# Attention scores and a chunk scan contracted over all 128 rows, with masks added by VectorE

## The chip, the cores and the metric

One core of a Trainium2 chip runs the whole kernel as one program. The metric is the device time of that program in microseconds (us), from its start to its end. A core has a matrix engine (TensorE, PE in the profile; its weight loads are PEld), three engines for element-wise work (VectorE or DVE, ScalarE or ACT, GpSimd or POOL), an engine that starts transfers (SyncE or SP), and DMA queues between the chip's memory (HBM) and the on-chip memories: SBUF, from which engines read and which has 128 rows (partitions), and PSUM, into which TensorE writes. A matrix multiplication on TensorE contracts over the rows: it takes a stationary operand (loaded as weights) and a moving one, both with the contracted index on the rows.

## The reference, cut to what matters

Two transformer blocks run one after the other on 256 tokens of width 1024, all in float32. Block 1 has two attentions side by side (branch a: 8 heads of width 64; branch b: 8 heads whose queries and keys are 96 wide), and a feed-forward layer that gathers experts. Block 2 has two layers: the first mixes tokens by a gated unit and a gated delta rule (a scan over 4 chunks of 64 tokens, 4 heads of width 128), the second by a differential attention: 8 heads, each with two maps of width 64, whose logits get a slope times the distance. What bears on the change:

```python
# branches a and b (one key block covers all 256 tokens)
s = einsum('bhqd,bhkd->bhqk', q, k) * scale
p = softmax(where(k_pos <= q_pos, s, -inf))          # then p @ v

# the differential attention
dist   = q_pos[:, None] - k_pos[None, :]
logits = einsum('bqhrd,bkhrd->bhrqk', q_blk, k) - slopes * dist     # slopes: 2 ** -(head + 1)
probs  = softmax(where(dist >= 0, logits, -inf))
attn   = probs[:, :, 0] - lam * probs[:, :, 1]       # then attn @ v

# one chunk of the scan
v_new = u_c - einsum('bhck,bhkv->bhcv', w_c, state)
o_c   = einsum('bhck,bhkv->bhcv', q_c, state) + einsum('bhij,bhjv->bhiv', qk_c, v_new)
state = state * gl_c + einsum('bhck,bhcv->bhkv', k_c, v_new)
```

## The kernel before, in words

The code is written stage by stage, and a tile framework orders each engine's instructions by its own cost model and by which buffers are free; `issue_after` holds an instruction back until another is issued. So the order on an engine isn't that of the code: between the attention heads TensorE also has passes of big matrix products (`gemm_steps`, whose float32 precision is made of three products of split weights, lines 83 to 85), and VectorE and ScalarE have the splits of their weights (lines 77 and 78). Two PSUM pools of four buffers feed this: `mm_tile` for scores and transposes, `acc_tile` for the products' sums.

**Scores.** The 256 queries make two tiles of 128. For a head, `scores` (lines 289 to 301) fills three blocks of 128 columns of one PSUM tile: queries 0 against keys 0, queries 1 against keys 0, queries 1 against keys 1. In branch a and the differential attention a head (or map) is 64 wide: two of them lie one above the other in the 128 rows of `qaT`, `kaT` and `qkT` (named `dT` in the profile), and a matmul (line 295) reads only the 64 rows of its own. In branch b the operands have 96 rows. The mask is added by a further matmul in bf16 (line 297): the identity times the mask (`identb`, `cmb`), and in the differential attention the identity times the head's slope (`idh`) times the distances (`cb`, named `c1bb` in the profile). VectorE takes the negated row maxima (lines 299 and 300), ScalarE the exponentials from PSUM with their sums (`exps`, lines 303 to 305), each followed by an instruction that reads the sum's accumulator. `pv` (lines 307 to 316) transposes the probabilities on TensorE (line 310), lets ScalarE copy them (line 312) and multiplies by the values (lines 313 to 315). One head is worked ahead: the scores of head h + 1 stand in front of the transposes of head h.

**Around the scores.** In branch a `transposes_a` writes q^T and k^T, each by one ScalarE copy for every two pairs of heads; branch b's are copied by VectorE (line 465). In the differential attention `head_tr` does it (lines 1306 and 1307), half of the heads before head 0 and half after head 1's scores; `head_s` forms both maps of a head and combines them on VectorE (lines 1346 to 1350).

**The scan.** Two tiles of 128 tokens hold the four chunks of 64. Chunk c reads rows `rw` (the upper or lower 64) of tile c // 2: line 1076 multiplies the state (128 rows), line 1081 makes the state's update over the 64 rows of the chunk, lines 1093 and 1094 make the chunk's output in turn over 128 rows and 64 rows, head by head. `kdec` (named `kd`) holds the scaled keys, one tile per 128 tokens, made by `scaled` (line 966) on ScalarE ahead of the scan, as are `kbg` and the others.

Of the kernel before, what the change touches and what calls it, by code (L numbers as in the profile page):

```python
# [40 lines left out]
C_CM, C_D0, C_D1 = 0, 128, 256  # L41
C1_COLS = 384
# [6 lines left out]
def kernel(ctx: ExitStack, tc: tile.TileContext, A: dict, out: bass.AP):  # L49
# [239 lines left out]
    def scores(qT, kT, name, masks, w):  # L289

        s = mm_tile(name + "s")
        for o, q, k in ((0, 0, 0), (1, 1, 0), (2, 1, 1)):
            c = slice(o * P, o * P + P)
            m = masks[o]
            PE.matmul(s[:, c], qT[:, q * P : q * P + P], kT[:, k * P : k * P + P], start=True, stop=m is None)
            if m is not None:
                PE.matmul(s[:, c], w, m, start=False, stop=True)
        nm = sm.tile([P, 2], F32, tag="nmx", name=name + "m")
        V.tensor_reduce(nm[:, 0:1], s[:, 0:P], AX.X, OP.max, negate=True)
        V.tensor_reduce(nm[:, 1:2], s[:, P : 3 * P], AX.X, OP.max, negate=True)  # L300
        return s, nm

    def exps(s, nm, p, sums):
        S.activation(p[:, 0:P], s[:, 0:P], AF.Exp, bias=nm[:, 0:1], accum_out=sums[:, 0:1])
        return S.activation(p[:, P : 3 * P], s[:, P : 3 * P], AF.Exp, bias=nm[:, 1:2], accum_out=sums[:, 1:2])
# [13 lines left out]
    with tc.tile_pool(name="p1", bufs=1) as p1:  # L319
# [13 lines left out]
        c1 = p1.tile([P, P], F32, name="c1")  # L333
        cmb = p1.tile([P, P], BF16, name="cmb")
# [33 lines left out]
        nc.sync.dma_start(c1, A["c1"][:, C_CM : C_CM + P])  # L368
        nc.sync.dma_start(fin, A["rows"][:, R_FIN : R_FIN + D].to_broadcast((P, D)))
        V.tensor_copy(cmb, c1)  # L370
# [48 lines left out]
        qaT = p1.tile([P, 4, T], F32, name="qaT")  # L419
        kaT = p1.tile([P, 4, T], F32, name="kaT")  # L420

        def transposes_a(i, dst, sc):
# [3 lines left out]
            for g in range(2):  # L426
# [5 lines left out]
                S.activation(dst[:, 2 * g : 2 * g + 2], tp.rearrange("p (j t) -> p j t", j=2), AF.Copy, scale=sc)  # L432

        transposes_a(0, qaT, 0.125)
# [16 lines left out]
        transposes_a(1, kaT, 1.0)  # L451
# [20 lines left out]
        def attention(br, fill):  # L472
# [3 lines left out]
            for h in range(8 + AHEAD):  # L476
                if h < 8:
                    if br == "a":
                        qT, kT = (z[h % 2 * 64 : h % 2 * 64 + 64, h // 2, :] for z in (qaT, kaT))
                    else:  # L480
                        qT, kT = qbT[:, h, :], kbT[:, h, :]
                    s, nm = scores(qT, kT, f"at{br}{h}", (cmb, None, cmb), identb)
                    p = p1.tile([P, 3 * P], F32, tag="p", name=f"p{br}{h}", bufs=AHEAD + 1)
                    last_exp[:] = [exps(s, nm, p, sums[:, h, :])]
# [269 lines left out]
    with tc.tile_pool(name="p3", bufs=1) as p3:  # L754
# [16 lines left out]
        def v4(ps):  # L771
            return ps.rearrange("p (h d) -> p h d", h=4)
# [184 lines left out]
        V.tensor_mul(beg, beta, egc)  # L957

# [76 lines left out]
        for t in range(2):  # L1035
            kdec.append(scaled(f"kd{t}", ktok[t], ekd[:, t]))
# [29 lines left out]
        for c in range(4):  # L1066
# [4 lines left out]
            else:  # L1071
# [18 lines left out]
            for hd in range(4):  # L1090
# [3 lines left out]
                PE.matmul(oh, qkD[t][rw, hd], vn[rw, hd], start=st is None, stop=True)  # L1094
# [65 lines left out]
    with tc.tile_pool(name="p4", bufs=1) as p4_:  # L1160
# [3 lines left out]
        qkT = [p4_.tile([P, 8, T], F32, name=f"dT{i}") for i in range(2)]  # L1164
# [84 lines left out]

        c1 = p4_.tile([P, C1_COLS], F32, name="c1b")  # L1250
        nc.sync.dma_start(c1, A["c1"])
# [4 lines left out]
        cb = p4_.tile([P, C1_COLS], BF16, name="c1bb")  # L1256
        idh = [p4_.tile([P, P], BF16, name=f"idh{i}") for i in range(8)]
# [41 lines left out]
        def head_tr(i, hf):  # L1299
            gain = aq if i == 0 else gcols[:, G_AK : G_AK + 1]  # L1300
            for g in range(2):
                tp = mm_tile(f"td{i}{hf}{g}")
                for j in range(2):
                    for t in range(2):
                        b = hf * 512 + (2 * g + j) * P
                        PE.transpose(tp[:, j * T + t * P : j * T + t * P + P], qk[i][t][:, b : b + P], ident)
                S.activation(qkT[i][:, hf * 4 + 2 * g : hf * 4 + 2 * g + 2], tp.rearrange("p (j t) -> p j t", j=2), AF.Copy,
                             scale=gain)
# [211 lines left out]
```

## Time and profile before

| what | value |
|---|---|
| median of three runs | 1772.1 us (1767.64 to 1775.27) |
| the profiled execution's own time | 1771.07 us |
| its span in the trace | 1769.3 us |
| mean granted clock of TensorE | .997 of full speed |
| TensorE busy | 1731.0 us, 98% of the span |
| VectorE busy | 1132.1 us, 64% |
| ScalarE busy | 876.1 us, 50% |
| GpSimd busy | 0.8 us, 10 instructions |
| moved by DMA | 321.28 MB, mean 182 GB/s |

An engine's busy time counts the instructions that work on data. Matmuls are pipelined: in a row of equal ones each starts before the one ahead has ended, so the duration of one is longer than the distance of two starts. A float32 matmul is recorded as two passes; "x2" in a row of the timeline means two records of one form that follow each other, and its duration goes from the first start to the last end. The stages of this case lie at about 72 to 96 us (branch a), 113 to 137 us (branch b), 1149 to 1169 us (scan) and 1467 to 1526 us (differential attention).

### The profile page before, as it was taken

How to read it: one execution, taken by the hardware profiler on the slowest of the kernel's cores; microseconds unless marked ns; L12 is line 12 of the kernel's file. 1: busy time of each engine (PE TensorE's matmuls, PEld its weight loads, DVE VectorE, ACT ScalarE, POOL GpSimd, SP SyncE). 2: the span in 40 equal slices, each digit the busy share in tenths (PEclk: the TensorE clock that was granted, in tenths of full speed). 3: DMA queues.
4: the chain of work that ended last, by engine and by line, in shares of the span. 5: the costliest groups of instructions: out<-in, count | busy, mean ns of one | idle time of the engine just before them, and what ended most of it. 6: DMA issues, size and time to landing. Idle time of an engine off the chain costs nothing.

```text
span 1769.3 us, 26510 instructions
## 1 busy us (share of the span) xinstructions
PE 1731.0 (98%) x10846; PEld 1508.3 (85%) x10846; DVE 1132.1 (64%) x1867; ACT 876.1 (50%) x1146; POOL 0.8 (0%) x10
## 2 busy tenths in 40 slices
PE   8999999999999999999999999999999999999998
PEld 7788899899999999998888887878998787689996
DVE  6646699999656565555555597656555666665555
ACT  5654544555444444444444477535444565454444
POOL 0000000000000000000000000000000000000000
PEclk9999999999999999999999999999999999999999
DMA  6424445477777777765555543215555552255552
GB/s 234 140 96 146 173 152 178 150 275 286 254 253 247 247 248 247 245 211 190 191 190 190 183 156 120 96 48 194 190 189 189 173 179 96 81 177 179 184 191 95
DMA packets 83066, 321.28 MB, mean 182 GB/s; under 512 B 9472, under 2 KB 44544, under 8 KB 47104
## 3 DMA queue, kind: packets, MB, share of 16 engines
q1 hardware_dynamic: 82944, 319.58, 53.0%
q8 instruction: 85, 1.39, 0.3%
q14 instruction: 37, 0.30, 0.0%
HBM read 301.72 MB, written 17.83 MB: 181 GB/s over the span
## 4 chain that ended last, share of the span: by engine, by line
PE 91%; DVE 5%; ACT 3%; DMA 1%; issue 1%; SPq 0%; DVEq 0%; ACTq 0%
PE pv L85 7%; PE pv L83 7%; PE pv L84 7%; PE m L84 3%; PE m L85 3%; PE m L83 3%; PE gp L717 2%; PE wia L84 1%; PE wia L85 1%; PE wia L83 1%; PE pt L92 1%; PE pj L1180 1%; PE wda L83 1%; PE wda L85 1%; PE wda L84 1%
## 5 line engine op out<-in xcount | busy, mean ns | idle before, releaser
L740 ACT ACTIVATE wh<-ga 128x512 fp32r<-128x512 f32 x64 | 40.4, 632 | 194.9 <-PE pv L84 194.9
L741 DVE TENSOR_TENSOR wl<-ga,wh 128x512 fp32r<-128x512 f32 x64 | 44.2, 693 | 91.6 <-ACT wh L740 91.6
L1200 ACT ACTIVATE ah<-mr 128x512 fp32r<-128x512 f32 x32 | 20.2, 631 | 76.8 <-DVE mr L1197 76.8
L712 DVE TENSOR_TENSOR oh<-oh,gT 128x1024 f16<-128x1024 f16 x64 | 42.3, 687 | 5.3 <-PE gp L717 5.3
L737 DVE TENSOR_TENSOR ga<-ga,gt 128x512 f32<-128x512 f32 x64 | 41.2, 686 | 5.5 <-DMA gt<-gd 5.4
L1201 DVE TENSOR_TENSOR al<-mr,ah 128x512 fp32r<-128x512 f32 x32 | 22.2, 692 | 21.6 <-ACT ah L1200 21.6
L720 ACT ACTIVATE stg<-gp 128x512 f32<-128x512 f32 x64 | 32.9, 608 | 0.0
L717 PE MATMUL gp<-oh,oh 128*128 128x128 f16 x512 | 32.5, 219 | 0.0
L717 PEld LDWEIGHTS <-oh 128*128 128x128 f16 x512 | 29.4, 97 | 0.8
L92 PE MATMUL pt<-c,x 128*128 128x128 f32 x128 | 21.7, 295 | 6.9 <-DMA x<-x 5.3
L92 PEld LDWEIGHTS pt<-c,x 128*128 128x128 f32 x128 | 16.1, 150 | 12.2 <-issue 6.3
L78 DVE TENSOR_TENSOR wiw_0l<-wiw,wiw_0h 128x2048 fp32r<-128x2048 f32 x7 | 16.0, 2291 | 11.5 <-ACT wiw_0h L77 11.5
L83 PE MATMUL wia<-wiw_0h,gh 128*128 128x512 f32 x56 | 22.6, 406 | 0.0
L84 PE MATMUL wia<-wiw_0l,gh 128*128 128x512 f32 x56 | 22.5, 402 | 0.0
L100 ACT ACTIVATE gh<-pt,gcols 128x256 fp32r<-128x256 f32 x32 | 13.0, 475 | 19.0 <-PE pt L92 19.0
L85 PE MATMUL wia<-wiw_0h,gl 128*128 128x512 f32 x56 | 22.3, 398 | 0.0
L709 DVE TENSOR_TENSOR oh<-iotaR,i1T 128x1024 f16<-128x1024 f16 x32 | 22.0, 686 | 0.2 <-PE gp L717 0.2
L84 PE MATMUL wia<-wiw_1l,gh 128*128 128x512 f32 x56 | 22.1, 394 | 0.0
L85 PE MATMUL wia<-wiw_1h,gl 128*128 128x512 f32 x56 | 22.0, 394 | 0.0
L1197 DVE TENSOR_TENSOR mr<-mr 128x512 f32<-128x512 f32 x32 | 21.9, 685 | 0.1
L83 PE MATMUL wia<-wiw_1h,gh 128*128 128x512 f32 x56 | 21.8, 389 | 0.0
L78 DVE TENSOR_TENSOR wdw_0l<-wdw,wdw_0h 128x2048 fp32r<-128x2048 f32 x6 | 13.8, 2293 | 12.2 <-ACT wdw_0h L77 11.9
(2913 smaller groups left out, 6689.7 us busy)
## 6 DMA issues: line engine op xcount, KB each, us to landing
u<-eu SPq DMA_DIRECT2D x64, 1024.0 KB, 5.0
v<-ev SPq DMA_DIRECT2D x64, 1024.0 KB, 4.9
m<-w_mlp SPq DMA_DIRECT2D x64, 1024.0 KB, 4.9
gd<-stg SPq DMA_DIRECT2D x16, 1024.0 KB, 3.9
gt<-gd SPq DMA_DIRECT2D x256, 64.0 KB, 4.5
wiw<-w_in SPq DMA_DIRECT2D x14, 1024.0 KB, 4.8
wdw<-w_qkv SPq DMA_DIRECT2D x12, 1024.0 KB, 4.8
q<-w_query SPq DMA_DIRECT2D x8, 1024.0 KB, 4.9
```

The lines of the kernel that those rows point to most:

```text
L78: V.tensor_sub(lo[:, :n], w[:, :n], hi[:, :n].bitcast(F32)),
L83: PE.matmul(o, ah, bh, start=start, stop=False)
L84: PE.matmul(o, ah, bl, start=False, stop=False)
L85: PE.matmul(o, al, bh, start=False, stop=stop)
L92: PE.transpose(pt[:, t * P : t * P + P], src[t][:, k * P : k * P + P], ident)
L712: V.tensor_tensor(oh[2 + i], oh[1], tok(gT[i]), OP.mult)
L717: PE.matmul(ps[:, i * P : i * P + P], oh[0][:, 2 * g + i // 2, :, i % 2], oh[2 + m][:, 2 * g + i // 2, :, i % 2], start=m == 0, stop=m == 1)
L720: S.activation(stg[:, :, c : c + 4], ps.rearrange("p (t n) -> p n t", t=4), AF.Copy, scale=2.0 ** -15)
L737: V.tensor_tensor(w4, w4, gts[q][:, :, 2 * jj : 2 * jj + 2, :].rearrange("p g j t -> p j g t"), OP.mult)
L740: S.activation(wh, w, AF.Copy)
L741: V.tensor_sub(wl, w, wh.bitcast(F32))
L1201: V.tensor_sub(al, r, ah.bitcast(F32))
```

## The change

There are three parts. First, `scores` makes two matmuls, of 128 and of 256 columns, both over all 128 rows in branch a and the differential attention. For this q^T is kept in two tiles: one has the upper heads' 64 rows and zeros below, the other the lower ones' and zeros above. GpSimd writes the zeros; ScalarE copies each half of a transpose's result to its own tile. k^T stays whole. Second, the masks are no matmuls: VectorE's `tensor_tensor_reduce` adds a float32 mask to the scores in PSUM, negates the sum, writes it to the tile in SBUF that will hold the probabilities, and forms the row minimum, which is the negated maximum. In the program this is one instruction and a second one that reads the accumulator. The exponential then runs in place with scale -1. In the differential attention GpSimd makes the head's mask (`ali`, 128 by 384) from the distances and the head's slope, in two alternating buffers. Third, `kdec` has three tiles, one per chunk that updates the state, whose other 64 rows are zero (the factors `ekc` are masked by columns of `blk`), and all matmuls and subtractions of the scan go over 128 rows.

```diff
-    def scores(qT, kT, name, masks, w):
+    def scores(qT, kT, name, mask, p):
         s = mm_tile(name + "s")
-        for o, q, k in ((0, 0, 0), (1, 1, 0), (2, 1, 1)):
-            c = slice(o * P, o * P + P)
-            m = masks[o]
-            PE.matmul(s[:, c], qT[:, q * P : q * P + P], kT[:, k * P : k * P + P], start=True, stop=m is None)
-            if m is not None:
-                PE.matmul(s[:, c], w, m, start=False, stop=True)
+        PE.matmul(s[:, 0:P], qT[:, 0:P], kT[:, 0:P], start=True, stop=True)
+        PE.matmul(s[:, P : 3 * P], qT[:, P : 2 * P], kT[:, 0 : 2 * P], start=True, stop=True)
         nm = sm.tile([P, 2], F32, tag="nmx", name=name + "m")
-        V.tensor_reduce(nm[:, 0:1], s[:, 0:P], AX.X, OP.max, negate=True)
-        V.tensor_reduce(nm[:, 1:2], s[:, P : 3 * P], AX.X, OP.max, negate=True)
-        return s, nm
+        for i, c in enumerate((slice(0, P), slice(P, 3 * P))):
+            V.tensor_tensor_reduce(p[:, c], s[:, c], mask[:, c], -1.0, 3.0e38, OP.add, OP.min, nm[:, i : i + 1])
+        return nm
-    def exps(s, nm, p, sums):
-        S.activation(p[:, 0:P], s[:, 0:P], AF.Exp, bias=nm[:, 0:1], accum_out=sums[:, 0:1])
...
+    def exps(nm, p, sums):
+        S.activation(p[:, 0:P], p[:, 0:P], AF.Exp, bias=nm[:, 0:1], scale=-1.0, accum_out=sums[:, 0:1])
...
-        c1 = p1.tile([P, P], F32, name="c1")
-        cmb = p1.tile([P, P], BF16, name="cmb")
+        c1 = p1.tile([P, 3 * P], F32, name="c1")
...
-        qaT = p1.tile([P, 4, T], F32, name="qaT")
+        qaT = [p1.tile([P, 4, T], F32, tag=("qaT", "yha")[i], name=f"qaT{i}") for i in range(2)]
+        for i in range(2):
+            GP.memset(qaT[i][64 - 64 * i : 128 - 64 * i], 0.0)
...
-                S.activation(dst[:, 2 * g : 2 * g + 2], tp.rearrange("p (j t) -> p j t", j=2), AF.Copy, scale=sc)
+                for r, d in dst:
+                    S.activation(d[r, 2 * g : 2 * g + 2], tp[r].rearrange("p (j t) -> p j t", j=2), AF.Copy, scale=sc)
...
+        for c in range(3):
+            V.tensor_scalar(ekc[:, c], ekd[:, c // 2], blk[:, c % 2 * 64 : c % 2 * 64 + 1], None, OP.mult)
...
-            kdec.append(scaled(f"kd{t}", ktok[t], ekd[:, t]))
+            for c in (0, 1) if t == 0 else (2,):
+                kdec.append(scaled(f"kd{c}", ktok[t], ekc[:, c], "de1" if c == 2 else None, 1 if c == 2 else 2))
...
-                V.tensor_tensor(vn[rw], us[t][rw], v4(vp)[rw], OP.subtract)
+                V.tensor_tensor(vn, us[t], v4(vp), OP.subtract)
...
-                    PE.matmul(sp_[:, hd * P : hd * P + P], kdec[t][rw, hd], vn[rw, hd], start=True, stop=True)
+                    PE.matmul(sp_[:, hd * P : hd * P + P], kdec[c][:, hd], vn[:, hd], start=True, stop=True)
...
-                PE.matmul(oh, qkD[t][rw, hd], vn[rw, hd], start=st is None, stop=True)
+                PE.matmul(oh, qkD[t][:, hd], vn[:, hd], start=st is None, stop=True)
...
+        for i in range(2):
+            GP.memset(qkT[i][64 - 64 * i : 128 - 64 * i], 0.0)
...
-        idh = [p4_.tile([P, P], BF16, name=f"idh{i}") for i in range(8)]
+        ali = [p4_.tile([P, 3 * P], F32, tag="ali", name=f"ali{i}", bufs=2) for i in range(8)]
...
-            V.tensor_copy(cb, c1)
-            for i in range(8):
-                V.tensor_scalar(idh[i], identb, 2.0 ** -(i + 1), None, OP.mult)
...
+            GP.tensor_scalar(ali[hd], c1, 2.0 ** -(hd + 1), None, OP.mult)
...
-                qT, kT = (z[r * 64 : r * 64 + 64, hd, :] for z in qkT)
-                s, nm = scores(qT, kT, f"ds{hd}{r}", [cb[:, m : m + P] for m in (C_D0, C_D1, C_D0)], idh[hd])
...
+                nm = scores(qkT[r][:, hd], qkT[2][:, hd], f"ds{hd}{r}", ali[hd], e)
```

The framework orders the engines anew. On TensorE, at the differential attention's head 2 before the change (`ds20s` are the scores of head 2's first map, `da0t` the transposes of head 0's probabilities, `wda` the passes of the product that makes queries, keys and values):

```order
L85 MATMUL wda_0_13833<-wdw_1h,bl 128x512
L310 MATMUL da0t<-c_70,de_13770 128x128
L295 MATMUL ds20s<-dT_11441,dT_11440 128x128
L310 MATMUL da0t<-c_70,de_13770 128x128 x2
L297 LDWEIGHTS idh_13232
L297 MATMUL ds20s<-c1bb,idh_13232 128x128
L295 MATMUL ds20s<-dT_11441,dT_11440 128x128
L297 LDWEIGHTS idh_13232
L297 MATMUL ds20s<-c1bb,idh_13232 128x128
L295 MATMUL ds20s<-dT_11441,dT_11440 128x128
L313 MATMUL oa_13847<-dv_13227,da0pT 128x128
```

and the same place on TensorE after it:

```order
L85 MATMUL wda_0_13780<-wdw_1h,bl 128x512
L306 MATMUL da0t<-c_70,de_13722 128x128
L292 MATMUL ds20s<-dT_11406,dT_11404 128x128
L293 MATMUL ds20s<-dT_11406,dT_11404 128x256
L306 MATMUL da0t<-c_70,de_13722 128x128 x2
L292 MATMUL ds21s<-dT_11406,dT_11405 128x128
L293 MATMUL ds21s<-dT_11406,dT_11405 128x256
L309 MATMUL oa_13794<-dv_13194,da0pT 128x128
```

The mask's matmuls and their weight loads are gone, and both maps' scores now stand ahead of head 0's product with the values. On VectorE, at the reductions of the same head before (`ds20m` holds the negated row maxima):

```order
L299 TENSOR_REDUCE ds20m<-ds20s 128x1
L300 TENSOR_REDUCE ds20m<-ds20s 128x1
L299 TENSOR_REDUCE ds21m<-ds21s 128x1
L300 TENSOR_REDUCE ds21m<-ds21s 128x1
L1346 RECIPROCAL drc_13885<-dsu_13858 128x4
```

and after (`ISA` is the fused operation with its mask `ali`, then its accumulator's read; `de` are the tiles that take the probabilities):

```order
L296 ISA de_13807,ds20m<-ds20s,ali_13198 128x128
L296 ISA ds20m 128x1
L296 ISA de_13807,ds20m<-ds20s,ali_13198 128x256
L296 ISA ds20m 128x1
L296 ISA de_13816,ds21m<-ds21s,ali_13198 128x128
L296 ISA ds21m 128x1
L296 ISA de_13816,ds21m<-ds21s,ali_13198 128x256
L296 ISA ds21m 128x1
L1346 RECIPROCAL drc_13825<-dsu_13805 128x4
```

Eight instructions stand where four did. On ScalarE, ahead of the scan, before (`kd` and `kbg` are scaled keys, `cs` the convolution's evacuations, `kqT` the copies of transposed keys and queries, `wuw` a weight that is split):

```order
L966 ACTIVATE kd_10629<-ktok_9736,ekd 128x128 x4
L839 ACTIVATE cs_10704<-cvb_10701,gcols 128x256 x2
L839 ACTIVATE cs_10779<-cvb_10776,gcols 128x256 x2
L966 ACTIVATE kbg_10801<-ktok_9735,beg 128x128 x3
L866 ACTIVATE kqT<-tq_10301 128x4x128
L966 ACTIVATE kbg_10801<-ktok_9735,beg 128x128
L866 ACTIVATE kqT<-tq_10308 128x4x128
```

and after:

```order
L966 ACTIVATE kd_10576<-ktok_9690,ekc 128x128 x4
L836 ACTIVATE cs_10668<-cvb_10665,gcols 128x256
L836 ACTIVATE cs_10743<-cvb_10740,gcols 128x256 x2
L966 ACTIVATE kbg_10765<-ktok_9690,beg 128x128 x4
L966 ACTIVATE kbg_10789<-ktok_9691,beg 128x128 x4
L77 ACTIVATE wuw_1h<-wuw_1_10898 128x2048
L863 ACTIVATE kqT<-tq_10260 128x4x128
```

The copies of the transposed queries moved behind all of `kbg` and a weight's split; on TensorE eighteen passes of `wua` now stand ahead of their transposes, eleven before. The order of the scan's matmuls is row for row the same.

## Rows read from the trace of the kernel before

**Rows 1.** The page: engines' busy time (share) and instructions; the chain's shares.

```profile
PE 1731.0 (98%) x10846; PEld 1508.3 (85%) x10846; DVE 1132.1 (64%) x1867; ACT 876.1 (50%) x1146; POOL 0.8 (0%) x10
...
PE 91%; DVE 5%; ACT 3%; DMA 1%; issue 1%; SPq 0%; DVEq 0%; ACTq 0%
```

**Rows 2.** Windows: stretch and length in us, engines' busy time, PEclk, DMA share, GB/s.

```profile
1149.00:1169.00 20.00, 20.00 (x121) 15.74 (x120) 9.91 (x26) 4.68 (x11) 0.00 (x0) 1.00 0.00 1
1467.00:1526.00 59.00, 58.86 (x298) 40.22 (x297) 35.27 (x117) 32.73 (x91) 0.00 (x0) 0.97 0.23 75
1511.00:1515.00 4.00, 4.00 (x13) 2.26 (x13) 3.72 (x16) 0.72 (x4) 0.00 (x0) 0.61 0.70 256
```

**Rows 3.** Timeline, TensorE, differential attention: start, us, engine, line, operation, out<-in, form.

```profile
1468.39 0.48 PE L295 MATMUL ds00s<-dT,dT 64*128 64x128 f32 x2
1468.81 0.23 PE L297 MATMUL ds00s<-c1bb,idh 128*128 128x128 bf16 x1
...
1470.12 0.48 PE L295 MATMUL ds01s<-dT,dT 64*128 64x128 f32 x2
```

**Rows 4.** Line L252 on TensorE: ns min/median/max, first and last start.

```profile
L252 PE MATMUL u0p<-xf,u x32: 377/379/379, 222.6 to 229.3; 128*128 128x256 f32 x32
```

**Rows 5.** Timeline, TensorE, branch a: a score tile and what follows.

```profile
74.19 0.49 PE L295 MATMUL ata2s<-kaT,qaT 64*128 64x128 f32 x2
...
75.48 0.39 PE L313 MATMUL ya<-va,ata0pT 128*128 128x64 f32 x2
```

**Rows 6.** Timeline, TensorE, branch b: the first two score tiles' beginnings.

```profile
113.59 0.38 PE L295 MATMUL atb0s<-kbT,qbT 96*128 96x128 f32 x2
...
114.43 0.44 PE L295 MATMUL atb1s<-kbT,qbT 96*128 96x128 f32 x2
```

**Rows 7.** Timeline, TensorE, scan: a 64-row run, an alternating block, a 128-row run.

```profile
1148.59 1.16 PE L1081 MATMUL stp<-uu,kd 64*128 64x128 f32 x8
...
1160.53 0.49 PE L1093 MATMUL op<-st,qd 128*128 128x128 f32 x2
...
1163.86 1.16 PE L1076 MATMUL vp<-st,wT 128*128 128x128 f32 x8
1164.85 0.39 PE L1093 MATMUL op<-st,qd 128*128 128x128 f32 x2
```

**Rows 8.** Timeline, VectorE: two-source operations (the first four from PSUM), then reductions.

```profile
1139.36 1.12 DVE L1125 SCALAR_TENSOR_TENSOR uv<-sp,gcols,uv 128x128 f32<-128x128 f32 x4
...
1478.26 0.35 DVE L1350 SCALAR_TENSOR_TENSOR de<-de,drc,de 128x128 f32<-128x128 f32 x1
...
1478.61 0.48 DVE L1350 SCALAR_TENSOR_TENSOR de<-de,drc,de 128x256 f32<-128x256 f32 x1
...
1483.30 0.29 DVE L299 TENSOR_REDUCE ds20m<-ds20s 128x1 f32<-128x128 f32 x1 [1.48 <-PE ds20s L297]
1483.51 0.41 DVE L300 TENSOR_REDUCE ds20m<-ds20s 128x1 f32<-128x256 f32 x1
```

**Rows 9.** Timeline, ScalarE: an accumulator's read and the exponential behind it.

```profile
1472.81 0.19 ACT L304 ACTIVATION_READ_ACCUMULATOR de<-ds00s,ds00m 128x1 f32 x1
1472.91 0.46 ACT L305 ACTIVATE de<-ds00s,ds00m 128x256 f32<-128x256 f32 x1
```

**Rows 10.** Timeline, TensorE: the differential attention's first transpose of probabilities.

```profile
1480.24 0.27 PE L310 MATMUL da0t<-c,de 128*128 128x128 f32 x1
```

**Rows 11.** Timeline, VectorE: a weight's split in the differential attention.

```profile
1507.60 2.28 DVE L78 TENSOR_TENSOR woow_0l<-woow,woow_0h 128x2048 fp32r<-128x2048 f32 x1
```

**Rows 12.** Waits of TensorE, 72 to 137 us: total us, times, longest.

```profile
PE atb0t L310 <- ACT pb L304: 1.2, 1, 1.2
```

**Rows 13.** Timeline, ScalarE, ahead of the scan: the second half of wuw's split.

```profile
1078.92 1.96 ACT L77 ACTIVATE wuw_1h<-wuw 128x2048 fp32r<-128x2048 f32 x1
```

**Rows 14.** Timeline, TensorE: four equal passes under a lower and under the full clock.

```profile
1512.09 3.52 PE L1180 MATMUL pj<-wpj,pw 128*128 128x512 f32 x4
...
1520.05 1.94 PE L1180 MATMUL pj<-wpj,pw 128*128 128x512 f32 x4
```

More of the change, by code (lines that the diff above doesn't have):

```diff
@@ L40 @@
 C0_COLS = 416
-C_CM, C_D0, C_D1 = 0, 128, 256
-C1_COLS = 384
+C_CM, C_D0, C_D1, C_D2 = 0, 384, 512, 640
+C1_COLS = 768
 C_TRI, C_BLK, C_STR, C_LVL = 0, 128, 256, 512
@@ L431, in transposes_a @@
                         PE.transpose(tp[:, j * T + t * P : j * T + t * P + P], qk1[t][:, c : c + P], ident)
-                S.activation(dst[:, 2 * g : 2 * g + 2], tp.rearrange("p (j t) -> p j t", j=2), AF.Copy, scale=sc)
-        transposes_a(0, qaT, 0.125)
+                for r, d in dst:
+                    S.activation(d[r, 2 * g : 2 * g + 2], tp[r].rearrange("p (j t) -> p j t", j=2), AF.Copy, scale=sc)
+        transposes_a(0, [(slice(64 * i, 64 * i + 64), qaT[i]) for i in range(2)], 0.125)
         for t in range(2):
@@ L478, in attention @@
                     if br == "a":
-                        qT, kT = (z[h % 2 * 64 : h % 2 * 64 + 64, h // 2, :] for z in (qaT, kaT))
+                        qT, kT = qaT[h % 2][:, h // 2, :], kaT[:, h // 2, :]
                     else:
                         qT, kT = qbT[:, h, :], kbT[:, h, :]
-                    s, nm = scores(qT, kT, f"at{br}{h}", (cmb, None, cmb), identb)
                     p = p1.tile([P, 3 * P], F32, tag="p", name=f"p{br}{h}", bufs=AHEAD + 1)
-                    last_exp[:] = [exps(s, nm, p, sums[:, h, :])]
+                    nm = scores(qT, kT, f"at{br}{h}", c1, p)
+                    last_exp[:] = [exps(nm, p, sums[:, h, :])]
                     ps[h] = p
@@ L957 @@
         V.tensor_mul(beg, beta, egc)
+        ekc = p3.tile([P, 2, 8], F32, tag="ba", name="ekc").rearrange("p a b -> p (a b)")[:, 0:12].rearrange("p (c h) -> p c h", c=3)
+        for c in range(3):
+            V.tensor_scalar(ekc[:, c], ekd[:, c // 2], blk[:, c % 2 * 64 : c % 2 * 64 + 1], None, OP.mult)
         wT, qkD, qdT, kdec, units = [], [], [], [], []
@@ L1163 @@
         bl = p4_.tile([P, 8, T], F32R, name="bl")
-        qkT = [p4_.tile([P, 8, T], F32, name=f"dT{i}") for i in range(2)]
+        qkT = [p4_.tile([P, 8, T], F32, name=f"dT{i}") for i in range(3)]
         def pp_load(layer):
@@ L1306, in head_tr @@
                         PE.transpose(tp[:, j * T + t * P : j * T + t * P + P], qk[i][t][:, b : b + P], ident)
-                S.activation(qkT[i][:, hf * 4 + 2 * g : hf * 4 + 2 * g + 2], tp.rearrange("p (j t) -> p j t", j=2), AF.Copy,
-                             scale=gain)
+                for r, d in [(slice(64 * z, 64 * z + 64), qkT[z]) for z in range(2)] if i == 0 else [(slice(0, P), qkT[2])]:
+                    S.activation(d[r, hf * 4 + 2 * g : hf * 4 + 2 * g + 2], tp[r].rearrange("p (j t) -> p j t", j=2), AF.Copy,
+                                 scale=gain[r])
         order = [(n, k) for ns in ((0, 2), (4, 1), (3,), (5,)) for k in range(2) for n in ns]
@@ L1445, in _consts @@
     c1 = np.zeros((P, C1_COLS), np.float32)
-    c1[:, C_CM : C_CM + P] = np.where(k <= q, 0.0, NEG)
-    c1[:, C_D0 : C_D0 + P] = np.where(k <= q, k - q, NEG)
+    for o in (0, 2 * P):
+        c1[:, C_CM + o : C_CM + o + P] = np.where(k <= q, 0.0, NEG)
+        c1[:, C_D0 + o : C_D0 + o + P] = np.where(k <= q, k - q, NEG)
     c1[:, C_D1 : C_D1 + P] = k - q - P
```

14 lines of the change are left out of this document (6 added, 8 removed).

## The prediction

> **What bounds the kernel now.** I read the page's busy shares first, then its chain of work that ended last, then busy time by stretch, then single timelines. TensorE (PE) is busy 98% of the span and makes up 91% of the chain [rows 1]: what shortens TensorE's own work shortens the kernel, until another engine is late. In the diff attention (1467 to 1526) and the scan (1149 to 1169) TensorE has no idle time to speak of, while VectorE (DVE) is busy 35.3 of 59 us and 9.9 of 20, and GpSimd (POOL) not at all [rows 2]. So the sum has two sides: what TensorE is spared, and what it will wait for once its neighbours have less time. The pitch, from one start to the next, is what an instruction costs on a full engine; its own duration overlaps the next.
>
> **What TensorE is spared.** A float32 matmul shows as two passes.
> - Diff attention, 16 tiles (8 heads, 2 maps). Two passes over 64 rows have a pitch of .42 us, the mask's matmul .16, and a whole tile takes 1470.12 - 1468.39 = 1.73 [rows 3]. The new tile is a matmul of 128 columns and one of 256, over 128 rows. A long run of passes over 128 rows and 256 columns took 6.7 us from its first start to its 32nd, 6.7/31 = .216 a pass [rows 4], so .43 for two. For 128 columns I take half of it, .22. Together .65; I use .66. Spared: 16 x (1.73 - .66) = 17.1.
> - Branch a, 8 tiles of 75.48 - 74.19 = 1.29 [rows 5]: 8 x .63 = 5.0. The second tile comes behind copies of VectorE that keep their pace, so I count seven: 4.4.
> - Branch b, 8 tiles of 114.43 - 113.59 = .84 [rows 6], already over 96 rows: 8 x .18 = 1.4.
> - Scan. Where passes over 128 and 64 rows alternate, 16 took 1163.86 - 1160.53 = 3.33; a run of 8 over 128 rows alone took .99 [rows 7]. So 16 cost 1.98 in the new form, and three chunks alternate: 3 x 1.35 = 4.1. A run of 8 over 64 rows alone shows 1.16, as the run over 128 does [rows 7]: it is the alternation that costs, not the 64 rows. No bf16 mask stands in the scan, so the .42 in the diff attention is likely of the same kind: each tile's half of the rows differs from the last and from the full-row work between.
> Sum 27.0. Bounds: if the .42 is not lifted, the first matmul stays at .42 and the second takes .64, which is a rival below; below .22 + .43 no row of these passes goes.
>
> **What VectorE gets.** Two reductions per tile leave. They begin .21 apart, and the larger takes about .31 of pitch (.41 long) [rows 8]: .52 a tile. A fused operation takes the place of each, and an accumulator read follows each. The trace has no such operation. Lower bound: as quick as the reductions, with reads for nothing. Nearest row: the scalar_tensor_tensor, which reads two tensors as well: .35 and .48 long, about .26 and .39 of pitch; the form that reads PSUM takes 1.12 for four, as quick [rows 8]. Upper bound: twice these pitches. For the read I take ScalarE's own, .19 long with a pitch of .10 [rows 9]. The likely tile is .26 + .39 + .20 = .85, .33 more; 16 of them give VectorE 35.3 + 5.3 = 40.6 us in a stretch that shrinks to 59 - 17 = 42 us. That is close to full: the cover is nearly gone, and this is where I expect loss.
>
> The Trainium skill, "Vector Engine (DVE) Microarchitecture Reference", section "Points that are easy to get wrong", says that a two-source operation with two SBUF sources that are not bf16 runs at half rate, because no read port is left for the accumulator. Rows 8 show two-source float32 operations without an accumulator only; here one source is in PSUM, so I read the rule as not applying, but if it does, this is the upper bound's case, rival (c).
>
> **What is given back.**
> - Diff attention, first transposes. They began at 1480.24 without a wait [rows 10]. Four tiles are ahead of them, so TensorE arrives some 4 x 1.07 sooner, about 1476.0. Head 0's combined probabilities were ready when the last scalar_tensor_tensor ended, at 1479.1 [rows 8]; ScalarE now has two more evacuations there (q^T goes to two tiles, 64 rows each) and VectorE four longer tiles, but the scores come a little sooner. I put them at about 1478: 2 us of wait. Once that has settled, the next is where the split of woow holds VectorE for 2.28 us in front of head 6's tile [rows 11]: I give 1.0. Total 3.0.
> - Branch a. Only one tile is worked ahead, TensorE comes two tiles sooner (1.3) to probabilities that come .33 later: bounds 0 and 1.6; I take 1.5. Branch b has a wait of 1.2 at its first transposes now [rows 12]; it grows by .33 and two tiles of .18: .7.
> - Ahead of the scan, ScalarE scales one more kd set, and a q/k transpose's copy now queues behind the rest of kbg and the 1.96 us split of wuw [rows 13]. Bounds 0 and 1.96; eighteen other matmuls stand ahead of it on TensorE, seven more than before, so 1.2.
> - Off TensorE's path: the eight small VectorE operations and casts that made the bf16 masks go, and three tiny ones for ekc come; the zeroing of the q^T halves is on GpSimd, which is idle there [rows 1, 2] and has it long before the tiles are filled. The mask of block 1 is loaded with 384 columns instead of 128 before anything needs it. Nothing counted.
> - GpSimd's mask tile (128x384, eight times) has no row: the page's ten operations average .08 [rows 1], a VectorE pass of 128x256 .48 [rows 8], so .7 for 384 columns at that pace. It has a head's time, 42/8 = 5.2 us, and two buffers; I count nothing up to 5.2.
> - The clock. In 1511 to 1515 the granted clock was .61 in the mean, so much of it at the lower level (1.2 of 2.4 GHz) [rows 2], and four matmul passes of the same form lasted 3.52 us there against 1.94 later, 1.6 more [rows 14]. TensorE was busy without a gap around it [rows 2]. Whether it comes back at another place I cannot tell: half of 1.6, a gain of .8.
>
> **Sum.** 27.0 - 3.0 - 1.5 - .7 - 1.2 + .8 = 21.4. The profiled execution took 1771.07 us (span 1769.3, 1.8 around it): 1749.7. The median of the three runs is 1.0 above it, so I say 1750.
>
> **Rivals.**
> (a) Nothing waits and the clock stays up: 27.0 + 1.6 = 28.6 spared, 1743. For it: in both stretches TensorE hardly waits now [rows 2]. Against: VectorE at 40.6 of 42 us. 12%.
> (b) The forecast, 48%, own range 1745 to 1756.
> (c) The fused operation runs at half rate. A tile takes 2 x .65 + .20 = 1.50 and VectorE needs 35.3 + 16 x .98 = 51 us in the diff attention, 9 more than TensorE: 1759. For it: no row has such an operation with an accumulator. Against: the PSUM form in rows 8 is not slower. 15%.
> (d) Each head's chain (scores, fused operation, read, exp, combination, transposes) is longer than what TensorE has beside it, and about .5 us is lost in each of 24 heads: 12 us, 1762. For it: only one head is worked ahead, and rows 12 show such a wait already. Against: seven of eight heads in branch b show none. 14%.
> (f) The change doesn't do what it says: the .42 is not of the row halves. A tile costs .42 + .64 = 1.06; the diff attention saves 16 x .67 = 10.7, branch a 1.8, branch b loses 1.8, the scan saves nothing: 10.7 less some 5 of the losses above, 1765. Against: rows 7. 5%.
> (e) Slower: GpSimd makes each head's mask tile later than TensorE comes to it. The scores then wait behind the fused operation for their PSUM buffers, and the head's period is GpSimd's time. It decides from 5.2 us an operation, eats the whole gain at 5.2 + 22/8 = 8, and at 9.5 gives 1750 + 8 x 4.3 = 1784. For it: not one GpSimd arithmetic row in the trace. Against: .7 us by VectorE's pace leaves a factor of seven. 6%.
> The Trainium skill, "GPSIMD Engine Reference", section "Performance versus the Vector engine", shows element-wise work at about half VectorE's speed; by that an estimate is some 1.4 us, and (e) would not occur. No run here shows it yet.
>
> **How the numbers follow.** What can be told from no change is about .5%, 8.9 us: faster is below 1763.2, slower above 1781. Faster: (a), (b), nearly all of (c) and over half of (d), .83. Same: the rest of (d), (f) and a corner of (e), .12. Slower: .05 of (e). The range 1742 to 1764 leaves out (e), most of (f), the late part of (d) and the quick part of (a), together under .2. With both unknown VectorE costs at their lower bounds the time is near (a), with both at the upper near (c).
>
> **What would show it.** Right: pitch from tile to tile on TensorE near .66 in the diff attention, 16 passes in a scan chunk near 2 us, fused operations of .35 and .5, a wait of about 2 us at the first transposes of the diff attention and little later. Wrong: fused operations of .6 or .9 and VectorE without a gap (c); a wait of TensorE in most heads (d); first matmuls of .42 still (f); VectorE waiting for GpSimd (e). Losses outside these four stretches would mean that I missed a step altogether.

## The result and the profile after

The changed kernel took 1745.05 us (median of four executions, 1743.89 to 1747.08), the one before 1773.37 (four, 1767.64 to 1775.27): ratio .9847, 95% interval .9821 to .9873, a gain of 1.5%, more than the .5% below which a change cannot be told from none. The forecast was 1750, with a range of 1742 to 1764. The profiled execution has a span of 1742.3 us, 27.0 less than before.

The page after, its busy shares and the chain's, answers to [rows 1]:

```profile
PE 1700.4 (98%) x10702; PEld 1491.7 (86%) x10702; DVE 1130.6 (65%) x1924; ACT 883.8 (51%) x1156; POOL 22.9 (1%) x22
...
PE 88%; DVE 7%; ACT 4%; issue 1%; DMA 1%; SPq 0%; DVEq 0%; ACTq 0%
```

TensorE has 30.6 us less work; of the chain, VectorE has gained two points and ScalarE one. The windows after (columns as in [rows 2]): a stretch that holds w_kv_up's product, and the diff attention.

```profile
66.00:72.00 6.00, 5.42 (x18) 3.88 (x19) 2.78 (x11) 5.47 (x12) 0.00 (x0) 0.72 0.52 182
1454.00:1500.00 46.00, 42.96 (x235) 32.96 (x234) 37.66 (x152) 36.32 (x98) 12.91 (x6) 1.00 0.30 104
```

TensorE now has 3 us idle in the diff attention, where it had .14, and VectorE is busy 82% of it. The clock's drop of 1511 to 1515 is gone, but there are new ones at 66 to 72 us (mean .72, so partly at the lower level) and between 113 and 120 (mean .76).

Where the 27 us came from, by the first start of a tile on TensorE in both traces:

| from the start to the first ... | after against before there | stage's own change | forecast |
|---|---|---|---|
| u0p (experts; behind branches a and b) | -2.9 | -2.9 | -3.6 |
| gp (behind the experts' selection) | -6.1 | -3.2 | 0 |
| stp (ahead of it the scan's preparation) | -5.8 | +.3 | +1.2 |
| m_00p (behind the scan) | -11.1 | -5.3 | -4.1 |
| m_10p (behind the diff attention) | -27.0 | -15.9 | -14.9 |

A second profile of the changed kernel (the run "changed kernel again" below) has -4.8, -3.2, +.2, -5.3 and -16.5 in the third column: the scan repeats, the diff attention nearly so, and the branches differ by 1.9 us. A second profile of the kernel before differs from the first by up to 1.3 us in a stage.

The timeline of TensorE after, at the diff attention's first tile; it answers to [rows 3]:

```profile
1457.06 0.39 PE L292 MATMUL ds00s<-dT,dT 128*128 128x128 f32 x2
1457.28 0.60 PE L293 MATMUL ds00s<-dT,dT 128*128 128x256 f32 x2
1457.71 0.38 PE L292 MATMUL ds01s<-dT,dT 128*128 128x128 f32 x2
```

.22 + .43 = .65, as the sum had it. VectorE's fused operations in the same place, which answer to [rows 8]:

```profile
1458.02 0.29 DVE L296 CUSTOM_DVE_ANT_0 de<-ds00s,ali 128x128 f32<-128x128 f32 x1 [1.14 <-PE ds00s L293]
1458.24 0.08 DVE L296 DVE_READ_ACCUMULATOR2_ANT ds00m<- 128x1 f32 x1
1458.24 0.42 DVE L296 CUSTOM_DVE_ANT_0 de<-ds00s,ali 128x256 f32<-128x256 f32 x1
1458.58 0.08 DVE L296 DVE_READ_ACCUMULATOR2_ANT ds00m<- 128x1 f32 x1
1458.58 0.29 DVE L296 CUSTOM_DVE_ANT_0 de<-ds01s,ali 128x128 f32<-128x128 f32 x1
```

They cost what the reductions did, .29 and .42, and the accumulator's read overlaps the next start: .56 a tile (1458.02 to 1458.58), not .85. The scan after, a block of 16 passes, against [rows 7]:

```profile
1147.51 0.39 PE L1094 MATMUL op<-st,qd 128*128 128x128 f32 x2
1147.73 0.39 PE L1095 MATMUL op<-vn,qkd 128*128 128x128 f32 x2
...
1149.29 1.06 PE L1077 MATMUL vp<-st,wT 128*128 128x128 f32 x8
```

1.78 us instead of 3.33. The waits of TensorE after, in branches a and b and in the diff attention (columns as in [rows 12]):

```profile
PE atb0t L306 <- ACT pb L300: 1.6, 1, 1.6
PE wka L83 <- ACT wkw_0h L77: 1.6, 1, 1.6
PE wka L84 <- DVE wkw_0l L78: 0.5, 1, 0.5
...
PE da0t L306 <- DVE de L1350: 1.7, 1, 1.7
PE da6t L306 <- DVE de L1350: 0.7, 1, 0.7
PE pj L1181 <- ACT pp L1182: 0.5, 1, 0.5
```

All but the first are new; the first was 1.2 [rows 12].

### The profile page after: what moved, and what is told of

It reads as the page before. It is cut to its first block, busy times and chain, and to the rows that moved or that the text cites. A ratio compares the mean times of both kernels' runs of the same rounds, so it can differ in the third digit from the quotient of the medians.

```text
span 1742.3 us, 26306 instructions
## 1 busy us (share of the span) xinstructions
PE 1700.4 (98%) x10702; PEld 1491.7 (86%) x10702; DVE 1130.6 (65%) x1924; ACT 883.8 (51%) x1156; POOL 22.9 (1%) x22
## 4 chain that ended last, share of the span: by engine, by line
PE 88%; DVE 7%; ACT 4%; issue 1%; DMA 1%; SPq 0%; DVEq 0%; ACTq 0%
PE pv L85 7%; PE pv L83 7%; PE pv L84 7%; PE m L85 3%; PE m L84 3%; PE m L83 3%; PE gp L714 2%; PE wia L84 1%; PE wia L85 1%; PE wia L83 1%; PE pt L92 1%; PE pj L1181 1%; PE wda L85 1%; PE wda L83 1%; PE wda L84 1%
```

## The experiments

**Theory 1:** TensorE loses about .2 us where a matmul over 64 rows stands beside one over 128 rows; both the full rows and the masks' leaving remove such neighbours. **Theory 2:** only the masks' leaving counts. **Theory 3:** a 64-row score matmul costs .42 whatever is beside it.

**Masks on VectorE, 64 rows kept** (no zero halves, scan as before; lines cut, against the changed kernel):

```diff
-        PE.matmul(s[:, 0:P], qT[:, 0:P], kT[:, 0:P], start=True, stop=True)
-        PE.matmul(s[:, P : 3 * P], qT[:, P : 2 * P], kT[:, 0 : 2 * P], start=True, stop=True)
+        for o, q, k in ((0, 0, 0), (1, 1, 0), (2, 1, 1)):
+            PE.matmul(s[:, o * P : o * P + P], qT[:, q * P : q * P + P], kT[:, k * P : k * P + P], start=True, stop=True)
...
-                nm = scores(qkT[r][:, hd], qkT[2][:, hd], f"ds{hd}{r}", ali[hd], e)
+                nm = scores(qkT[0][r * 64 : r * 64 + 64, hd], qkT[1][r * 64 : r * 64 + 64, hd], f"ds{hd}{r}", ali[hd], e)
```

> The kernel before with the masks on VectorE alone: score matmuls stay over 64 rows (three of 128 columns), no mask matmuls, the scan as before. Theory 1 (TensorE loses about .2 us where a matmul over 64 rows stands beside one over 128 rows or the other 64, and nothing within a run of one kind): a tile of three pairs costs 3 x .22 plus one switch in and one out, .9 to 1.05 us instead of 1.73; diff attention 16 x .75 = 12 less, branch a 2.4, branch b 1.4, waits take 3 back: about 1760. Theory 2 (the gain is that the masks left TensorE, rows don't matter): tile .66, about 1753. Theory 3 (a 64-row score matmul costs .42 whatever stands beside it): tile 1.26, about 1766.

Measured: 1757.13 (1749.57 to 1764.43, six executions), ratio .9918 (.9891 to .9946). That lies between what theories 1 and 2 expected, so the time alone does not decide. The diff attention became 16.9 us shorter than before (by the table's marks), one more than in the changed kernel. TensorE's timeline there:

```profile
1478.65 0.27 PE L293 MATMUL ds01s<-dT,dT 64*128 64x128 f32 x1
1478.65 0.27 PE L293 MATMUL ds00s<-dT,dT 64*128 64x128 f32 x1
1478.76 0.27 PE L293 MATMUL ds01s<-dT,dT 64*128 64x128 f32 x1
1478.76 0.27 PE L293 MATMUL ds00s<-dT,dT 64*128 64x128 f32 x1
```

Two passes of one map follow each other .11 apart (ds00s at 1478.65 and 1478.76), so a pair takes .22: nothing of the .42 is left, and theory 3 falls. Two passes of the other map, which lies on the other half of the rows, start at the same moments. The Trainium skill, "TensorEngine Tiling (Array Packing)", section "Tiling Modes", says that tiles of 64 rows work independently of each other, and that a change of the tiling mode (not of the tile) drains the engine; the trace agrees with both halves, by the equal starts here and by a pair's .42 in [rows 3] against .22. The recorded theory 1 also counted a loss between the two halves of the rows; the rows show none, and the two tiles take 1.20 together (1478.10 to 1479.30) where .9 to 1.05 each was expected. But in branch a the clock fell, in the window of this run from 82 to 92 us:

```profile
82.00:92.00 10.00, 10.00 (x33) 7.63 (x33) 1.69 (x9) 2.84 (x13) 0.00 (x0) 0.50 0.29 105
```

TensorE is busy throughout at 1.2 GHz. The spread goes with the clock: of its six executions the two with a mean clock of .997 and .999 took 1750.8 and 1749.6, the two at .989 and .990 took 1764.4 and 1761.9.

**Full rows, masks on TensorE in bf16** (scan, reductions and exponentials as before; the lines of `scores` alone, against the changed kernel):

```diff
-        PE.matmul(s[:, 0:P], qT[:, 0:P], kT[:, 0:P], start=True, stop=True)
-        PE.matmul(s[:, P : 3 * P], qT[:, P : 2 * P], kT[:, 0 : 2 * P], start=True, stop=True)
+        PE.matmul(s[:, 0:P], qT[:, 0:P], kT[:, 0:P], start=True, stop=False)
+        PE.matmul(s[:, 0:P], w, masks[0], start=False, stop=True)
+        PE.matmul(s[:, P : 3 * P], qT[:, P : 2 * P], kT[:, 0 : 2 * P], start=True, stop=False)
+        n = masks[1].shape[-1]
+        PE.matmul(s[:, 3 * P - n : 3 * P], w, masks[1], start=False, stop=True)
```

> The kernel before with full-row score matmuls alone (128 and 256 columns, q^T in two zero-filled tiles), the masks still added by bf16 matmuls on TensorE (one of 128 and one of 256 columns; 128 and 128 in the branches), reductions and exponentials from PSUM as before, the scan as before. Theory 1: a tile is .65 + .06 + .11 = .82; diff attention 16 x .91 = 14.6 less, branch a 4.2, and 2.9 lost before w_kv_up and about 1.5 at the first transposes: about 1759. Theory 2: one mask matmul less per tile, .16 x 16 = 2.6 and the same losses: no gain, 1772.

Measured: 1754.02 (1751.06 to 1757.3), ratio .9915 (.9887 to .9942). The diff attention is 14.4 us shorter. Its first tile on TensorE:

```profile
1462.90 0.39 PE L292 MATMUL ds00s<-dT,dT 128*128 128x128 f32 x2
1463.12 0.22 PE L293 MATMUL ds00s<-c1bb,idh 128*128 128x128 bf16 x1
1463.18 0.65 PE L294 MATMUL ds00s<-dT,dT 128*128 128x256 f32 x2
1463.66 0.27 PE L296 MATMUL ds00s<-c1bb,idh 128*128 128x256 bf16 x1
1463.77 0.39 PE L292 MATMUL ds01s<-dT,dT 128*128 128x128 f32 x2
```

A pair of passes in front of a bf16 mask over the same rows costs .22, the mask .06: theory 2 falls, and theory 1 is left. The tile is .87 (.82 expected). The run's time is below both expectations, 5 us under theory 1's and 18 under theory 2's. So either part of the score change alone takes most of the diff attention's gain (16.9 and 14.4); together they give 15.9.

**The scan alone.** The kernel before with the scan's lines of the change.

> The kernel before with the scan's part of the change alone. Theory 1: three chunks' output blocks fall from 3.33 to about 1.8 us, the scan is 5 us shorter, .3 lost ahead of it: 1768. Theory 2 (rows don't matter): 1773 as before.

Measured: 1767.01 (1760.27 to 1770.41, ten executions), ratio .9973 (.9954 to .9991). In its trace the stage from stp to m_00p is 5.3 us shorter, as in the changed kernel. The end result is less than that, and goes with the clock: the executions at .998 took 1760.3 and 1762.3 (the kernel before at .998, beside them: 1766.2 to 1768.8), the others, at .993 to .996, 1766.3 to 1770.4. In the profiled one 2.7 us were lost ahead of the scan, where .3 was expected and the clock has a mean of .83 from 1050 to 1070, and 2.4 in the diff attention, where this kernel is the one before:

```profile
1460.00:1524.00 64.00, 64.00 (x312) 44.64 (x310) 36.93 (x121) 33.91 (x94) 0.00 (x0) 0.92 0.23 76
```

**How near is VectorE to its limit?** The changed kernel with each fused operation twice:

```diff
-            V.tensor_tensor_reduce(p[:, c], s[:, c], mask[:, c], -1.0, 3.0e38, OP.add, OP.min, nm[:, i : i + 1])
+            for _ in range(2):
+                V.tensor_tensor_reduce(p[:, c], s[:, c], mask[:, c], -1.0, 3.0e38, OP.add, OP.min, nm[:, i : i + 1])
```

> The changed kernel with each fused VectorE operation and its accumulator read issued twice (the same result): .56 us more on VectorE per tile, 9 us in the diff attention, where the trace shows 37.7 busy of 46. If VectorE is as close to its limit there as the prediction held: 4 to 6 us slower than 1745, 1749 to 1751. If TensorE's other work covers it: within 2 us, 1745 to 1747.

Measured: 1757.91 (1756.23 to 1758.49), 13 us above the changed kernel: more than either expectation. The diff attention is 9.9 us longer, by more than VectorE's added 9. Its waits and its window:

```profile
PE wda L84 <- DVE wdw_1l L78: 3.2, 1, 3.2
PE da5t L307 <- DVE de L1351: 1.8, 1, 1.8
PE oa L310 <- ACT da5pT L309: 0.6, 1, 0.6
PE ds60s L292 <- DVE ds50m L297: 0.5, 1, 0.5
PE oa L310 <- ACT da6pT L309: 0.4, 1, 0.4
```

```profile
1454.00:1512.00 58.00, 51.23 (x243) 37.76 (x242) 49.75 (x224) 38.28 (x99) 7.55 (x6) 0.91 0.29 103
```

These are 6.5 us of waits, and the clock falls to a mean of .91. TensorE's idle time grows from 3.0 to 6.8 us and the lower clock takes about 5 (.09 of 58 us): VectorE had little room left, and by this estimate about half of the loss comes by the clock and not by the waits. The rest of the 13 us lies outside this stage. An operation at half rate would have added at least as much to VectorE's work, so the 9 us of the prediction's rival (c) were not too many.

**The wait at w_kv_up.** The changed kernel with half of branch a's q^T copied by VectorE:

```diff
-                for r, d in dst:
-                    S.activation(d[r, 2 * g : 2 * g + 2], tp[r].rearrange("p (j t) -> p j t", j=2), AF.Copy, scale=sc)
+                for n, (r, d) in enumerate(dst):
+                    o, z = d[r, 2 * g : 2 * g + 2], tp[r].rearrange("p (j t) -> p j t", j=2)
+                    if n == 0:
+                        S.activation(o, z, AF.Copy, scale=sc)
+                    else:
+                        V.tensor_scalar(o, z, sc, None, OP.mult)
```

> The changed kernel with the second half of branch a's q^T copied by VectorE instead of ScalarE (two operations), nothing else. If the extra ScalarE copies are what delayed the split of w_kv_up (2.1 us of waits and passes at the lower clock behind them, 2.9 in all): the first w_kv_up pass comes without a wait and the kernel is 2 to 3 us quicker than the changed one, 1742 to 1743. If the wait only moves to VectorE: within 1 us of it, 1745.

Measured: 1744.73 (1739.61 to 1745.76), ratio .9845 (.9816 to .9874). The waits of TensorE there:

```profile
PE ata1t L306 <- ACT pa L300: 1.0, 1, 1.0
PE wka L83 <- ACT qb L441: 0.6, 1, 0.6
```

The wait at w_kv_up is .6 instead of 2.1, but 1.0 is new at branch a's transposes of probabilities, so the wait has partly moved. u0p starts 4.3 us sooner than in the changed kernel's first trace, but only 2.4 sooner than in its second, and the granted clock of 1.00 from 60 to 72 us stands in that second trace as well. The profiled execution lost the gain again in the experts' selection (a wait of 3.0 at tsel and a mean clock of .83 from 332 to 342) and ahead of the scan (3.4 us between gp and stp with a clock of .74 from 1050 to 1070, where the same code in the mixed kernel below lost .4 at a clock of 1.00). By the times the step is not shown to be worth anything.

**Full rows or 64 rows.** The changed kernel with its two score matmuls over 64 rows, once timed and once more for a second profile:

```diff
-                        qT, kT = qaT[h % 2][:, h // 2, :], kaT[:, h // 2, :]
+                        qT, kT = (z[h % 2 * 64 : h % 2 * 64 + 64, h // 2, :] for z in (qaT, kaT))
...
-                nm = scores(qkT[r][:, hd], qkT[2][:, hd], f"ds{hd}{r}", ali[hd], e)
+                nm = scores(qkT[0][r * 64 : r * 64 + 64, hd], qkT[1][r * 64 : r * 64 + 64, hd], f"ds{hd}{r}", ali[hd], e)
```

> The changed kernel without its full-row score matmuls: masks on VectorE, two score matmuls of 128 and 256 columns over 64 rows as q^T and k^T lie, no zero halves, no extra copies; the scan as changed. If full rows bring nothing once the masks are off TensorE: 1742 to 1745, and no wait at the diff attention's first transposes. If full rows keep the clock up in branch a (in the run with vector masks over 64 rows the granted clock was .50 to .52 from 82 to 106 us): several of the executions lose 5 to 13 us there, median 1750 with a spread of over 8.

> The kernel with score matmuls over 64 rows, masks on VectorE and the new scan once more, for a second profile: its five executions ran at mean clocks of .998 to .990 and the profiled one was the best. If the lost clock lies in branch a: a granted clock of about .5 for some 10 us or more between 72 and 110 us. If it lies elsewhere, the windows show where.

Measured: 1751.46 (1745.67 to 1756.95, mean clocks .998 to .990), ratio .9896 (.986 to .9932), 6.2 above the changed kernel beside it on the same chip (1745.24); the second profile's execution took 1751.81. The first profile fell on the best execution and has no drop. Of the second one, branch a:

```profile
72.00:82.00 10.00, 9.23 (x38) 6.00 (x37) 5.50 (x16) 6.28 (x19) 0.00 (x0) 0.71 0.35 124
82.00:92.00 10.00, 10.00 (x34) 7.20 (x33) 4.14 (x13) 2.86 (x11) 0.00 (x0) 0.50 0.29 105
```

It ends branch a 7 us later than the first. Two of three profiles with 64-row scores and no mask matmuls show this drop; of seven profiles with full-row scores none does (clock 1.00 from 82 to 92 in each), nor do the three of the kernel before and of the scan alone, whose 64-row matmuls have full-row masks between them. So the second expectation is borne out for branch a, on few profiles; what brings the clock down in one execution and not in another stays open. In the diff attention the 64 rows did not bring the clock down (1.00 in all three profiles), and the first transposes wait for nothing.

**The likely best of both:** branch a as in the run with half of q^T on VectorE, the diff attention over 64 rows.

> The likely best of both: branch a over full rows with half of q^T copied by VectorE, the diff attention over 64 rows with whole q^T and k^T tiles, masks on VectorE, the scan as changed. If both local findings hold and add up (2.5 from w_kv_up, 1.7 from the first transposes' wait): 1741 us. If the diff attention's 64 rows bring the clock down as in branch a: 1746 or more, with a larger spread.

> The changed kernel once more, beside the three above on the same chip: 1745 if the first figure holds; its routing stage should again be 3 us shorter than in the one trace of before (wait of 1.6 instead of 3.4 at tsel).

Measured on one chip: the mixed kernel 1741.04 (1738.41 to 1744.61, six executions), ratio .9832 (.9803 to .9862); the changed kernel again 1745.24 (1741.44 to 1751.57, six), ratio .9864 (.9835 to .9894). The mixed kernel has 4 us less in the medians, with ranges that overlap: it is the better of the two, most likely, but not beyond what the measurement can tell. The kernel before took 1770.09 beside them (twelve executions), so on this chip the change gained 24.9 us.

**GpSimd's mask tile.** The changed kernel with each made four times:

```diff
-            GP.tensor_scalar(ali[hd], c1, 2.0 ** -(hd + 1), None, OP.mult)
+            for _ in range(4):
+                GP.tensor_scalar(ali[hd], c1, 2.0 ** -(hd + 1), None, OP.mult)
```

> The changed kernel with each head's mask tile computed four times by GpSimd (the same result). In the trace of the changed kernel one such operation takes 1.2 us, or 3.1 where a weight's split on VectorE runs beside it, and the head's period in the diff attention is 43/8 = 5.4 us. By the prediction's rival on GpSimd it decides from about 5.2 us a head: four take 4.8 alone and 5 to 9 with the splits, so some heads wait and the kernel is 3 to 10 us slower, 1748 to 1755. If the two buffers let GpSimd run far enough ahead, or the scores aren't held by it: 1745.

Measured: 1748.79 (1746.94 to 1755.16), ratio .9878 (.9842 to .9915), in the diff attention 5.8 us longer than the changed kernel. GpSimd's timeline, and VectorE's wait for it:

```profile
1472.83 4.93 POOL L1340 TENSOR_SCALAR ali<-c1b 128x384 f32<-128x384 f32 x4 [0.64 <-DVE ds21m L296]
1478.93 18.62 POOL L1340 TENSOR_SCALAR ali<-c1b 128x384 f32<-128x384 f32 x12 [1.17 <-DVE ds31m L296]
...
DVE de L296 <- POOL ali L1340: 1.7, 2, 1.0
```

From 1478.9 it works without a gap for three heads, 6.2 us each, and for the last two of them VectorE waits for it. The head of 4.9 us causes no wait, so the rival's point of 5.2 us fits. How much of the 5.8 us that makes is not shown: the clock was also lower, .93 in the mean from 1454 to 1506, which is up to 3.6 us. The change itself uses 1.2 to 3.2 us a head.

**Is the gain in the experts' selection the change's?** The kernel before once more:

> The kernel before once more, for a second profile. If the 3.4 us wait of tsel on VectorE and the passes at the lower clock behind it (expert selection, 336 to 347 us) were chance of one execution: the stage from u12p's first pass to the first gp pass takes 8 us as in the changed kernel, and the span is near 1766. If the kernel before has it always: 11 us.

Measured: 1770.74, span 1768.9. Here the expectation of chance is not borne out for the kernel before: both of its profiles have the long form. The rows are TensorE's waits at tsel in the first profile of before, after, and in the run of the scan alone:

```profile
PE tsel L687 <- DVE pf L674: 3.4, 1, 3.4
```

```profile
PE tsel L684 <- DVE pf L671: 1.6, 1, 1.6
```

```profile
PE tsel L687 <- DVE pf L674: 1.6, 1, 1.6
```

The second profile of before has 2.9 there. But the run of the scan alone has the same instructions in block 1 as the kernel before, in the same order on TensorE, VectorE and ScalarE, and it has the short form; and the run with half of q^T on VectorE, with full rows, has the long one (3.0). In the three long ones ScalarE waits for a transfer, the load of u12, here in the first profile of before:

```profile
318.70 1.92 ACT L77 ACTIVATE u12h<-u 128x2048 fp32r<-128x2048 f32 x1 [1.85 <-DMA u<-eu]
```

VectorE's split and the selection behind it then come later (by 1.9 us in that profile, against the scan alone), TensorE's wait grows, and the passes behind it run at a lower clock (a mean of .58 from 340.5 to 344.5 in before). So these 3 us are not the change's arithmetic. Of the ten profiles with new score code nine have the short form, of the three with the old code one; why the transfer is late in some executions, and whether the change makes that rarer, stays open.

## Why the prediction was right, point by point

- **TensorE's spared time.** Right for the tiles: .65 in the diff attention against the .66 counted, and .65 to .76 in branch a. That the .42 comes of the change between 64 and 128 rows, argued from [rows 7], was shown by the two runs that undo one part each. A tile on the other half of the rows than the last, which the prediction named beside it, costs nothing. What the sum did not see: the two parts of the score change are nearly alternatives. The step was sized for both at once, so the total is not hurt.
- **The scan** was mis-sized: 4.1 counted, 5.3 measured. The sum took 1.98 for 16 passes from a run that stood between rows of the other kind [rows 7]; in the new block a pair of passes has a pitch of .22, so 16 take 1.78, and chunk 0 and the updates became quicker too.
- **VectorE** was mis-sized upward: .85 a tile counted, .56 measured, since the fused operations keep the reductions' pace. The half rate that the Trainium skill gives ("Vector Engine (DVE) Microarchitecture Reference", section "Points that are easy to get wrong") is for two sources in SBUF; with one in PSUM, as here, it doesn't show.
- **What is given back.** The first transposes of the diff attention: 2 us counted, 1.7 measured, .7 and .5 later where 1.0 was counted, and the clock's gain was the whole 1.6, not half. That is the 1.0 by which this stage beat the sum. The prediction gave two reasons for the first wait, ScalarE's extra copies of q^T and VectorE's longer tiles; only the first holds. Head 0's fused operations had ended by 1459.14, and its exponentials began at 1463.21, behind the copies. ScalarE's timeline after, and in the run over 64 rows, which has no such wait:

```profile
1459.12 2.77 ACT L1307 ACTIVATE dT<-td,aq 64x512 f32<-64x512 f32 x4
...
1460.32 1.25 ACT L1302 ACTIVATE dT<-td,aq 128x512 f32<-128x512 f32 x2
```

  Ahead of the scan .3 was lost and not 1.2: the waits at the k and q transposes are 1.5 together, against 1.6 before.
- **Branch a** has a step that was wrong in its place: the loss was put at the first transposes of probabilities (1.5); it came earlier, where the prediction had not looked. The copies of q^T in two halves take ScalarE 2.40 us where two copies took 1.09, and the split of w_kv_up is queued behind them; before, its first half also stood ahead of the last piece of qb. ScalarE's timeline before (the first two rows) and after:

```profile
59.78 1.09 ACT L432 ACTIVATE qaT<-tqa 128x512 f32<-128x512 f32 x2
63.34 0.64 ACT L77 ACTIVATE wkw_0h<-wkw 128x512 fp32r<-128x512 f32 x1
...
60.09 2.40 ACT L429 ACTIVATE qaT<-tqa 64x512 f32<-64x512 f32 x4
62.52 1.09 ACT L429 ACTIVATE kaT<-tqa 128x512 f32<-128x512 f32 x2
63.49 2.00 ACT L437 ACTIVATE qb<-wqa,rqr 128x384 f32<-128x384 f32 x4
65.35 1.18 ACT L77 ACTIVATE wkw_0h<-wkw 128x512 fp32r<-128x512 f32 x2
```

  It cost 2.1 us of waits, and the window of 66 to 72 above shows the lower clock behind them: w_kv_up's last pass starts 2.9 later than before. The same waits stand in the second profile of the changed kernel and in that with GpSimd's mask made four times, but there the clock is 1.00 from 66 to 72, and u0p starts 1.9 and 2.6 us sooner than in the first. So the place of the loss was wrong, while the branches' 3.6 us lie within what the three profiles show (2.9 to 5.5 against the first profile of before). The prediction had weighed those extra copies in the diff attention alone. In branch b the first transposes' wait grew by .4, where .7 was counted.
- **The rivals.** (a) was near in time (1743) by other terms: the waits came nearly as counted, but the selection's 3.2, the scan's 1.2 more and .8 of clock were added. (c) and (e) did not occur; the run with each fused operation twice shows TensorE waiting for VectorE, that with four masks VectorE waiting for GpSimd at 6.2 us a head. A mask takes GpSimd 1.2 to 3.2 us, not the .7 counted, and that is still under 5.2. (d) did not: TensorE waits at three heads of 24. (f) is refuted.
- **The sum.** 1749.7 and the 1.0 above it make 1750.7, not 1750. Of the 5.6 us between 21.4 and 27.0, 3.2 are the experts' selection, 1.2 the scan, 1.0 the diff attention, .9 the scan's preparation, and -.7 the branches. The 3.2 are luck: no term stood for them, and without them the gain of the profile is 23.8. The other differences are terms that were mis-sized, and they nearly all fell on the same side.

## What to carry to other kernels

Where matmuls over half of the rows alternate with matmuls over all of them, look at the pitch of each pair before counting passes: making neighbours alike gives back what switching costs (here .2 us for each pair of passes), and it is enough to remove one of the two kinds. Which of them is not the same to the clock: with 64-row scores alone it fell in branch a in two of three profiles. Before a copy is split in two by rows (here the halves took as long as the wholes, on ScalarE), follow its engine's queue and see which weight or transfer is prepared behind it; the price shows there and not at the operation's reader. A wait of TensorE of a microsecond or two can cost again as much in passes at the lower clock (it did in one of the two profiles of the changed kernel), and a wait moved is not a wait removed.

## What was not expected of the hardware

- 64-row passes on different halves of the rows can start together (1478.65 twice); two maps over 64 rows are as quick as over zero-filled 128 (1.20 us against two tiles of .65).
- In branch a, 64-row scores without full-row masks between them ran at a granted clock of .50 from 82 to 92 us in two of three profiles, with TensorE busy 100%; with full rows it was 1.00 in all seven.
- GpSimd's 128x384 multiply takes 1.2 us, but 3.1 to 3.2 where VectorE subtracts two SBUF tensors, as here from 1459.14 for 2.29 us:

```profile
1459.38 3.08 POOL L1339 TENSOR_SCALAR ali<-c1b 128x384 f32<-128x384 f32 x1 [269.31 <-DVE ds01m L296]
1463.52 1.18 POOL L1339 TENSOR_SCALAR ali<-c1b 128x384 f32<-128x384 f32 x1 [1.07 <-DVE dr11z L116]
```

  The long one ends 1.03 us behind the subtraction, about its own length without company. The Trainium skill, "SBUF — State Buffer", section "Who interferes with whom", says that such an operation and a GpSimd one that reads SBUF shut each other out; the trace agrees.
